# A transpose whose stores write every eighth group of four columns instead of 512 neighbouring ones

## The chip, the cores and the metric

The kernel runs on one NeuronCore of a Trainium2 chip. The metric is the device time of one execution in microseconds, lower is better. The profiled times below come from one execution recorded by the hardware profiler.

## The reference

The input is a matrix of 8192 by 8192 float32 numbers, 256 MiB. The output is its transpose.

```python
def setup_inputs():
    return {"x": np.random.randn(8192, 8192).astype(np.float32)}

def reference(x):
    return np.transpose(x)
```

Every element is read once and written once: 268.4 MB in, 268.4 MB out.

## The kernel before

**Tiling.** The input is cut into two stripes of J = 4096 columns, and each stripe into CH = 64 chunks of P = 128 rows. A chunk is thus 128 x 4096 floats, 2 MB: one row of x per partition, 16 KB each. The 128 chunks (`chunks`, line 98) are worked through in order, first all of stripe 0, then all of stripe 1.

**Loading.** `load(t)` (line 100) brings chunk t into one of three buffers `in0` to `in2`. The first three loads are issued from SP, all later ones from ACT, once PE has finished with the chunk that was in the buffer (lines 242 and 243).

**Transposing.** `transposes(k)` (line 111) works on buffer k with TensorE (PE). A chunk is divided into NR = 8 *ranges*, and each range into B = 4 transposes of 128 x 128 floats. Line 120 says which 128 columns of the chunk one transpose takes: in range q, transpose b takes the columns q * 512 + b, q * 512 + 4 + b, q * 512 + 8 + b and so on. A range is therefore 512 neighbouring columns, and after its four transposes partition p of PSUM holds the four neighbouring columns q * 512 + 4p to q * 512 + 4p + 3, 128 values of each. PSUM is used in two halves of four ranges, `ps0` and `ps1`; PE waits at line 116 until a half has been emptied, and runs in a loop of its own ("turns").

**Copying.** ACT empties the first half (ranges 0 to 3) and DVE the second (ranges 4 to 7) by copies at line 228 into blocks of the tensor `regs`. There are NREG = 9 blocks. A block holds a *window*: one range over up to W = 8 chunks in a row, so that each partition has 4 rows of the output with up to 8 * 128 = 1024 floats (4 KB) of each. The windows of the eight ranges are staggered by one chunk, so that as a rule one block becomes full with every chunk. Before a block is used again, the engine that fills it waits for the store that empties it (line 202).

**Storing.** `store(q, e, count)` (line 160) writes a full block to the output, 2 MB as a rule, with one DMA issued from ACT (line 28, inside the helper `wide_dma`; the very first store goes through line 174). Lines 166 to 168 say where. The output is a matrix of 8192 rows of 32 KB. Column j of x is row j of the output. Partition p writes the rows j0 + 4p to j0 + 4p + 3, with j0 the first column of the range. Neighbouring partitions write 4 rows, 128 KB, apart. At the passage from stripe 0 to stripe 1 a window has two parts, and its store is issued as two DMAs, one for each stripe's rows.

**Order.** ACT's instruction stream holds, for each chunk, its own copies, the stores of both halves and one load, in the order written. All of these DMAs go into one queue (q10). SP issues nothing after the first three loads and waits for the last stores at the end (line 245).

Of the kernel before, what the change touches and what calls it, by code (L numbers as in the profile page):

```python
# [24 lines left out]
def wide_dma(nc, eng, queue, out, in_):  # L25


    return eng.add_instruction(
        mybir.InstDMACopy(
            mode="Copy",  # L30
            name=nc.get_next_instruction_name(),
            engine=eng.engine,
            ins=[physical(in_)],
            outs=[physical(out)],
            queue=queue,
        )
    )
# [3 lines left out]
def kernel(  # L41
# [14 lines left out]
    P = 128  # L56
# [4 lines left out]
    S = 32  # L61
    B = 4
# [5 lines left out]
    J = S * P  # L68

    with tc.tile_critical():  # L70
        nc.alloc_sbuf_tensor("pad", [P, 32], dt)
        ident = nc.alloc_sbuf_tensor("ident", [P, P], dt).ap()
        ins = [nc.alloc_sbuf_tensor(f"in{k}", [P, J], dt).ap() for k in range(NIN)]
# [15 lines left out]
            out=ident,  # L89
# [21 lines left out]
        def transposes(k):  # L111
            nc.tensor.sem_inc(s_ld[k], -16).wait_op(s_ld[k], 16, "sem-ge")
            for q in range(NR):
                e, g = divmod(q, NH)
                if g == 0:
                    nc.tensor.sem_inc(s_bank[e], -1).wait_op(s_bank[e], 1, "sem-ge")  # L116
                for b in range(B):
                    tr = nc.tensor.transpose(  # L118
                        pss[e][:, (g * B + b) * P:(g * B + b + 1) * P],
                        ins[k][:, q * B * P + b:(q + 1) * B * P - B + b + 1:B],  # L120
                        ident,
                    )
                if q % 2:
                    tr.then_inc(s_pe, 1)
# [13 lines left out]
        with nc.body("turns", valid_engines=pe):  # L138
            now = nc.snap(turn, min_val=0, max_val=T // NIN)
            with nc.tensor.If(now < 3):  # L140
                hint = nc.tensor.mark_branch_hint_location()
            with nc.tensor.If(now > 0):
                transposes(NIN - 1)
            for k in range(NIN - 1):
                transposes(k)
            nc.regs_alu(turn, turn, 1, op=mybir.AluOpType.add)
            nc.tensor.br_lt(
                turn, T // NIN + 1, on_true="turns", on_false="done"
            ).branch_hint(hint)
# [10 lines left out]
        def store(q, e, count):  # L160
            t0, r, parts = window.pop(q)
            nc.scalar.wait_ge(s_cp[e], count)
            base = 0
            for s, a, z in parts:
                rows = (z - a) * P
                j0 = s * J + q * B * P
                dst = out[j0:j0 + B * P, a * P:a * P + rows]
                dst = dst.rearrange("(q b) i -> q b i", q=P)
                src = regs[:, r * SIZE + base:r * SIZE + base + B * rows]
                base += B * rows  # L170
                if any(stored):
                    st = wide_dma(nc, nc.scalar, "qActDynamicHW", dst, src)
                else:
                    st = nc.scalar.dma_start(
                        out=dst, in_=src.rearrange("q (b i) -> q b i", b=B)
                    )
                st.then_inc(s_st[r], 16)
                stored[r] += 1
            free.append(r)
# [5 lines left out]
        for t, (s, c) in enumerate(chunks):  # L185
            for e in range(2):
# [3 lines left out]
                for q in range(e * NH, (e + 1) * NH):  # L190
# [13 lines left out]
                    k = [p[0] for p in parts].index(s)  # L204
                    base = r * SIZE + B * P * sum(z - a for _, a, z in parts[:k])
                    _, a, z = parts[k]
# [13 lines left out]
                for u in runs:  # L220
                    off, dist = place[u[0]]
                    gap = place[u[-1]][0] - place[u[-2]][0] if len(u) > 1 else 0
                    dims = [list(regs.ap[0]), [gap, len(u)], [dist, B], [1, P]]
                    o = bass.AP(regs.tensor, regs.offset + off, dims)
                    i = pss[e][:, u[0] * B * P:(u[-1] + 1) * B * P]
                    i = i.rearrange("p (l b i) -> p l b i", b=B, i=P)
                    eng.wait_ge(s_pe, t * NH + (e * NH + u[-1]) // 2 + 1)  # L227
                    cp = nc.scalar.copy(out=o, in_=i) if e == 0 else nc.vector.tensor_copy(out=o, in_=i)  # L228
                    ends = [e * NH + g for g in u if closes(window[e * NH + g], t)]
                    if ends:  # L230
                        cp.then_inc(s_cp[e], 1)
                        copied[e] += 1
                    if u is runs[-1]:
                        if ends:
                            eng.wait_ge(s_cp[e], copied[e])
                            eng.sem_inc(s_bank[e], 1)
                        else:
                            cp.then_inc(s_bank[e], 1)
                    for q in ends:
                        store(q, e, copied[e])  # L240
# [35 lines left out]
```

## Time and profile before

| what | value |
|---|---|
| median of 3 runs | 1263.84 us (1263.76 to 1263.89) |
| span of the profiled execution | 1261.2 us |
| bytes moved by DMA | 536.97 MB |
| loads: number, size, us from issue to landing | 125 (from ACT), 2048 KB, 21.7 |
| full stores: number, size, us from issue to landing | 114, 2048 KB, 17.5 |
| copies on ACT: number, busy us | 256, 251.3 |
| copies on DVE: number, busy us | 250, 302.7 |
| DVE's idle time until PE was done | 780.2 us |
| granted TensorE clock, mean | 0.751 |

A span is the time from the first to the last instruction of the profiled execution; the times of the runs are measured around the whole execution and lie a little above it. "Busy" is the time in which an engine executes instructions; for the DMA engines it is the time their packets took. A packet is the piece of a transfer that one of the core's 16 DMA engines moves in one go; for a full load or store here it is the 16 KB of one partition. Times "to landing" count from the DMA's issue until its semaphore reports that the data has arrived, so they contain the time in the queue.

### The profile page before, as it was taken

The page shows a single profiled execution, that of the slowest core. Times are in us where ns is not written, and L with a number is a line of the kernel's source. Part 1 is how long each engine was busy: PE and PEld are TensorE (multiplying, and loading weights), DVE is VectorE, ACT ScalarE, POOL GpSimd, SP SyncE. Part 2 cuts the span into 40 slices and gives each one's busy share as a digit, 9 for nine tenths or more (in the row PEclk, how much of TensorE's full clock was granted, in tenths as well). Part 3 has the DMA queues.
Part 4 walks back from the last instruction along what each step waited for, and adds up shares of the span by engine and source line. Part 5 has one row for each costly group of instructions (what it writes and reads, how often), then busy time and mean ns, then how long its engine had stood idle before and what let it go on. Part 6 is the DMA issues. An engine that isn't in the chain of part 4 may idle for free. (4 is left out here: it accounts for less than half of the span.)

```text
span 1261.2 us, 9840 instructions
## 1 busy us (share of the span) xinstructions
PE 740.3 (59%) x4096; PEld 719.8 (57%) x4096; DVE 302.7 (24%) x250; ACT 252.6 (20%) x257; POOL 0.7 (0%) x6
## 2 busy tenths in 40 slices
PE   6555655665556565665555655656566655656561
PEld 6555555665556555655555655656566655656561
DVE  3322222222222222222222222222222222222220
ACT  3212121121111211122211121121111211122120
POOL 0000000000000000000000000000000000000000
PEclk9987867777776868687776777676867677777866
DMA  9999999999999999999999999999999999999998
GB/s 386 429 427 426 430 427 429 431 428 430 431 428 431 429 429 430 430 429 430 425 423 419 431 430 429 430 430 429 431 430 429 431 429 430 430 430 429 429 429 351
DMA packets 39273, 536.97 MB, mean 426 GB/s; under 512 B 4320, under 2 KB 4832, under 8 KB 6240
## 3 DMA queue, kind: packets, MB, share of 16 engines
q10 hardware_dynamic: 38832, 530.60, 98.9%
q1 hardware_dynamic: 432, 6.29, 1.2%
q14 instruction: 8, 0.07, 0.0%
q8 instruction: 1, 0.02, 0.0%
HBM read 268.44 MB, written 268.44 MB: 426 GB/s over the span
## 5 line engine op out<-in xcount | busy, mean ns | idle before, releaser
L118 PE MATMUL ps<-ident,in 128*128 128x128 f32 x4096 | 740.3, 363 | 492.9 <-PEq L116 492.9
L118 PEld LDWEIGHTS ps<-ident,in 128*128 128x128 f32 x4096 | 719.8, 220 | 513.2 <-issue 513.2
L228 DVE COPY regs<-ps 128x512 f32<-128x512 f32 (+3 forms) x250 | 302.7, 1246 | 932.4 <-PE ps L118 780.2
L228 ACT COPY regs<-ps 128x512 f32<-128x512 f32 (+3 forms) x256 | 251.3, 1015 | 980.9 <-PE ps L118 495.5
L228 ACT ACT_TABLE_LOAD x1 | 1.3, 1283 | 0.9 <-SPq L70 0.9
L88 POOL TENSOR_SCALAR_AFFINE_SELECT ident<-ident 128x128 f32<-128x128 f32 x1 | 0.3, 292 | 0.2 <-POOL ident L86 0.2
L86 POOL MEMSET ident<- 128x128 f32 x1 | 0.2, 204 | 0.5 <-SPq L70 0.5
L260 POOL MEMSET const-bfloat16-1.0<- 128x1 bf16 x1 | 0.1, 101 | 0.0
L260 POOL MEMSET const-uint8-127<- 128x1 uint8 x1 | 0.1, 101 | 0.0
L260 POOL MEMSET const-float32-0.0<- 128x1 f32 x1 | 0.1, 98 | 0.2 <-issue 0.2
L260 POOL MEMSET const-float32-1.0<- 128x1 f32 x1 | 0.1, 98 | 0.0
## 6 DMA issues: line engine op xcount, KB each, us to landing
in<-in_x_dram ACTq DMA_DIRECT2D x125, 2048.0 KB, 21.7
out_dram<-regs ACTq DMA_DIRECT2D x114, 2048.0 KB, 17.5
out_dram<-regs ACTq DMA_DIRECT2D x4, 1792.0 KB, 17.1
in<-in_x_dram SPq DMA_DIRECT2D x3, 2048.0 KB, 11.6
out_dram<-regs ACTq DMA_DIRECT2D x4, 1536.0 KB, 15.2
out_dram<-regs ACTq DMA_DIRECT2D x4, 1280.0 KB, 15.5
out_dram<-regs ACTq DMA_DIRECT2D x4, 1024.0 KB, 15.6
out_dram<-regs ACTq DMA_DIRECT2D x4, 768.0 KB, 16.5
```

Source lines behind the costliest of these rows:

```text
L86: nc.gpsimd.memset(ident, 0.0).then_inc(s_id, 1)
L88: nc.gpsimd.affine_select(out=ident, in_=ident, compare_op=mybir.AluOpType.not_equal, fill=1.0, base=0, pattern=[[-1, P]], channel_multipl ...
L118: tr = nc.tensor.transpose(pss[e][:, (g * B + b) * P:(g * B + b + 1) * P], ins[k][:, q * B * P + b:(q + 1) * B * P - B + b + 1:B], ident,)
L228: cp = nc.scalar.copy(out=o, in_=i) if e == 0 else nc.vector.tensor_copy(out=o, in_=i)
L260: nc = _bacc.Bacc("TRN2", target_bir_lowering=False, num_devices=1)
```

## The change

Which columns form a range is changed. Before, range q was the columns q * 512 to q * 512 + 511 of the stripe. After, it is every eighth group of four columns: partition p gets the columns p * 32 + 4q to p * 32 + 4q + 3. The step between the columns of one transpose goes from B = 4 to S = 32. The destination of the stores changes with it: neighbouring partitions write 32 rows of the output, 1 MB, apart instead of 4 rows, 128 KB. With eight partitions for each of 16 DMA engines, neighbouring engines' rows lie 8 MB apart instead of 1 MB. The four rows that one partition writes are still neighbours. The order of the work, the sizes of all instructions and transfers, the buffers and the semaphores are as before.

```diff
@@ -117,7 +117,7 @@
                 for b in range(B):
                     tr = nc.tensor.transpose(
                         pss[e][:, (g * B + b) * P:(g * B + b + 1) * P],
-                        ins[k][:, q * B * P + b:(q + 1) * B * P - B + b + 1:B],
+                        ins[k][:, q * B + b:J - S + q * B + b + 1:S],
                         ident,
                     )
                 if q % 2:
@@ -163,9 +163,8 @@
             base = 0
             for s, a, z in parts:
                 rows = (z - a) * P
-                j0 = s * J + q * B * P
-                dst = out[j0:j0 + B * P, a * P:a * P + rows]
-                dst = dst.rearrange("(q b) i -> q b i", q=P)
+                dst = out[s * J:(s + 1) * J, a * P:a * P + rows]
+                dst = dst.rearrange("(p j) i -> p j i", p=P)[:, q * B:(q + 1) * B, :]
                 src = regs[:, r * SIZE + base:r * SIZE + base + B * rows]
                 base += B * rows
                 if any(stored):
```

## The prediction

> **What bounds the kernel now.** I began with the page's busy rows, its row of slices and its DMA rows, because they say at once which resource has no idle time.
>
> ```profile
> span 1261.2 us, 9840 instructions
> PE 740.3 (59%) x4096; PEld 719.8 (57%) x4096; DVE 302.7 (24%) x250; ACT 252.6 (20%) x257; POOL 0.7 (0%) x6
> DMA  9999999999999999999999999999999999999998
> GB/s 386 429 427 426 430 427 429 431 428 430 431 428 431 429 429 430 430 429 430 425 423 419 431 430 429 430 430 429 431 430 429 431 429 430 430 430 429 429 429 351
> DMA packets 39273, 536.97 MB, mean 426 GB/s; under 512 B 4320, under 2 KB 4832, under 8 KB 6240
> q10 hardware_dynamic: 38832, 530.60, 98.9%
> HBM read 268.44 MB, written 268.44 MB: 426 GB/s over the span
> ```
>
> No compute engine is busy for more than 59% of the span. The 16 DMA engines are: digit 9 in every slice but the last, and q10, the queue that ACT issues on, alone fills 98.9% of 16 engines for the whole span. The rate stands at 427 to 431 GB/s in nearly every slice. Exactly half of the bytes are written, so half of the engines' time belongs to the stores this change moves.
>
> The chain of waits is of little use here: it reaches back over the last 2% only. So I read the waits, the forms and two stretches instead.
>
> ```profile
> ACT regs L228 <- DMA out_dram<-regs: 473.9, 60, 10.4
> PE ps L118 <- PEq L116: 492.9, 127, 8.5
> L118 PE MATMUL ps<-ident,in 128*128 128x128 f32 x4096 | 740.3, 363 | 492.9 <-PEq L116 492.9
> 300.00:600.00 300.00, 179.58 (x981) 174.55 (x979) 73.81 (x62) 59.80 (x55) 0.00 (x0) 0.74 1.01 430
> 670.00:690.00 20.00, 12.02 (x64) 11.70 (x64) 4.77 (x5) 3.73 (x2) 0.00 (x0) 0.67 1.01 414
> ```
>
> The first line: ACT, about to fill a register block again, waits 473.9 us in all for the store that empties it. The second: PE waits 492.9 us at line 116, the wait for a free half of PSUM. Line 116 is held by the copies, the copies by the stores. Everything queues behind DMA. The two stretches (engine times, then clock, DMA share, GB/s) show the DMA engines full at 430 GB/s in the steady part, and full but slower, 414 GB/s, at 670 to 690 us, where the kernel passes from the first stripe to the second.
>
> The single packet records of the trace give the price of a transfer. There are 30976 records of 16384 bytes on the two kernel queues, which is 1936 for each of 16 engines, with a mean of 614.3 ns. In the stretch 300 to 600 us their mean is 613.1 ns, and nearly all are exactly 611 or 616 ns: an engine moving at its own pace, with memory never holding it up. At 670 to 690 us the mean is 645.7 ns, because 40 of 256 records are stretched. Over the whole execution 322 records exceed 620 ns; they average 766 ns and the longest is 1689 ns. So a packet can be held up in this kernel, but it is now rare.
>
> **The change part by part.** Nothing is added or removed: 142 stores, 128 loads, 4096 transposes and 506 copies stand in the same order with the same sizes and waits. Two address patterns move.
>
> 1. Line 120, the read of the input by the transposes. The step between two columns of one transpose goes from 4 elements (16 bytes) to 32 (128 bytes). The trace has no row with a step of 128 bytes. Lower bound: 0, the 363 ns of the row stay. What hides a dearer one: in the timeline around 600 us a chunk begins every 9.76 us (600.50, 610.24, 619.99, 629.76) and its 32 transposes occupy 5.05 to 6.33 us, so about 4 us per chunk are free. The load of a later chunk is issued only when PE is done with the buffer, but a load lands 21.7 us after its issue, while 2 MB at 430 GB/s take only 4.9 us; some 16 us of queueing lie between. If the transposes became 2 us dearer per chunk, loads would be issued 2 us later into a queue that is still full. Upper bound: twice the present time, 11.2 us per chunk, past the 9.76 us cover; that is a rival below. I take 0, since at either step each column read is a place of its own.
>
> 2. Lines 166 to 168, the destination of the stores. A store writes, from each of 128 partitions, 4 neighbouring rows of the output, 4 KB of each row (8 chunks of 128 floats); a row of the output is 32 KB. Two neighbouring partitions now write 4 rows, 128 KB, apart; after the change 32 rows, 1 MB, apart. With 128 partitions over 16 engines, 8 each, neighbouring engines go from 1 MB to 8 MB apart. Source, packet sizes and number of packets stay. So the only thing that can change is how long a store packet takes at the memory. There are 268.44 MB of stores, worth 268.44e6 / 16384 / 16 = 1024 full packets per engine. As the engines have no idle time, 1 ns on each store packet is 1.02 us on the span; there is no cover at all.
>
> No row of this trace has stores 8 MB apart, so I bound the price. From below: the records can at most all fall to the steady value, 614.3 - 612.9 = 1.4 ns on 1936 packets, a gain of 2.7 us; if the third of them at 616 ns also fell to 611, 3.2 us more. I see nothing that would make them do that, but 6 us is the most there is to gain. From above: every store packet as long as the mean stretched one, 766 - 613 = +153 ns, or +157 us. The longest record would give +1100 us, but one record in 30976 is no price for all. Between them I take the row that is nearest in kind: the stretch 670 to 690 us, full queues, steady work, but another set of addresses in flight (pieces for rows of both stripes, 4096 rows or 128 MB apart, beside loads of the second). There the mean packet was 645.7 - 613.1 = 32.6 ns longer. 1024 x 32.6 ns = +33 us. I choose a price above 0 because this stretch shows that a packet's time depends on which addresses are in flight together, and the change moves the addresses of every store, to distances whose low bits are all alike.
>
> The Trainium skill, page "DMA: Bandwidth & Descriptors", section "Latency and other measured facts", speaks against this change: in copies of 128 partitions with 16 KiB each, a distance between partitions of 512 KiB gave 207 GB/s per direction, 2 MiB 164, 4 and 8 MiB 103, and a pad of 4 KiB restored 214. The 1 MiB of the changed kernel lies between its first two figures; by them, an estimate, a store packet would take 613 x 214/207 = 634 to 613 x 214/164 = 800 ns, and the span grow by 21 to 191 us. No run here shows it yet; the present 128 KB at 430 GB/s does not contradict it.
>
> Sum: 0 for line 120, +33 us for the stores, on the profiled execution's 1261.2 us: 1294.6 us. The median of the runs, 1263.84 us, is 2.6 us above that span, so I add 2.6: 1297 us.
>
> **The rivals.**
>
> *Same.* The store packets keep their 611 to 616 ns, because an engine's own pace stays the limit. For it: nearly every record of the steady part is at one of two values, so memory has some room, of unknown size; and the four rows of a packet are still 32 KB apart, and the engines are at different points of their packets, which spreads the addresses. Against it: the stretched records show that the room ends somewhere. It decides as long as the mean store packet grows by less than 2.5 ns (0.2% of 1264 us over 1024 packets). Time: 1264 us. Here belongs also that the change does not do what it says: the trace does not show which rows an engine writes, and if packets were dealt out to the engines otherwise, the distance between engines would not be what the words say. The time would be the same 1264 us.
>
> *Every store packet is held up.* All of them behave like the 322 stretched ones: +157 us, 1261.2 + 157 + 2.6 = 1420 us. For it: the distances are all powers of two, so that whatever makes two engines meet makes many meet, and always. Against it: the distance before is a power of two as well, and costs nothing. The rule of the Trainium skill quoted above leads to a time between this one and my forecast.
>
> *PE becomes the bound.* The read with 128 byte steps is slower. It decides from 9.76 us per chunk, 1.7 times the present 5.6 us. At twice: 128 x 11.2 = 1434 us; with the 8.4 us before the first transpose and the 28 us after the last (1232.9 us) 1470 us. For it: PE is the second busiest engine. Against it: a step of 16 bytes already reads scattered columns.
>
> *Faster.* The few stretched packets (70 to 230 us, mean 615.1 ns) go away: 2.7 us, 1261 us; no more than 6 us.
>
> **How the numbers follow.** Forecast, a moderate stretch around 1297 us (1267 to 1350): 0.50. Same: 0.21. Every store held up, 1350 to 1450 us: 0.20. PE bound: 0.04. Faster by over 0.2% (what a measurement of this kernel can tell from no change, 2.5 us): 0.05. So slower 0.50 + 0.20 + 0.04 = 0.74. The range runs from 1262 us, which holds the unchanged time, to 1410 us, which takes in most of the way to the case of every store held up. The likeliest case's own range is 1267 to 1350 us.
>
> **What would show it.** If I am right, the DMA digits stay at 9 in all slices while the GB/s fall from 430 to about 418 in all of them, by the same share from the first store to the last; the records of 16384 bytes are no longer all at 611 and 616 ns, and the long ones are stores; stores take longer than 17.5 us to land and ACT waits more than 473.9 us for them; the 363 ns of the transposes stay as the clock allows. I am wrong if the GB/s stay at 430 (same), if the long packets are loads, if the loss sits in a few slices only, or if the DMA digits fall while PE's rise to 9 (the read of line 120).

## The result and the profile after

The changed kernel takes 1269.62 us (median of 6 runs, 1267.28 to 1275.23) against 1263.91 us (6 runs, 1263.76 to 1264.81) for the one before. The ratio is 1.0050, 95% interval 1.0031 to 1.0069. It is slower by 5.7 us, as the sign of the forecast said, but the forecast was +33 us; that is six times too much. The changed kernel also scatters over 8 us, the one before over 1 us in these six runs; in later series single runs of the kernel before reach 1268.8 and 1277.1 us.

The page of the changed kernel, in the rows that were shown of before:

```profile
span 1266.7 us, 9840 instructions
PE 736.2 (58%) x4096; PEld 715.5 (56%) x4096; DVE 302.7 (24%) x250; ACT 253.0 (20%) x257; POOL 0.7 (0%) x6
DMA  9999999999999999999999999999999999999998
GB/s 361 391 421 428 430 429 429 428 430 430 428 430 429 429 430 429 429 429 430 429 422 420 431 429 428 428 429 430 430 429 428 429 427 429 428 430 428 424 425 361
DMA packets 39273, 536.97 MB, mean 424 GB/s; under 512 B 4320, under 2 KB 4832, under 8 KB 6240
q10 hardware_dynamic: 38832, 530.60, 98.9%
HBM read 268.44 MB, written 268.44 MB: 424 GB/s over the span
```

The DMA engines are as full as before, the bytes and packets are the same, and the span is 1266.7 us instead of 1261.2 us. The place of the loss is in the row of GB/s: 361, 391, 421 in the first three slices, where before there were 386, 429, 427; from the fourth slice on the row is nearly that of before. The two waits, and the group of the transposes:

```profile
PE ps L118 <- PEq L116: 502.7, 126, 8.5
ACT regs L227 <- DMA out_dram<-regs: 476.7, 60, 10.6
```

```profile
L118 PE MATMUL ps<-ident,in 128*128 128x128 f32 x4096 | 736.2, 363 | 502.7 <-PEq L116 502.7
```

ACT waits for its stores 476.7 us instead of 473.9 us, PE waits for PSUM 502.7 us instead of 492.9 us, and a transpose still takes 363 ns. Full stores land in 17.5 us, as before. Next the first 100 us in three stretches (columns: stretch, its length, busy us and number of PE, PEld, DVE, ACT, POOL, clock, DMA share, GB/s). First the kernel before:

```profile
0.00:30.00 30.00, 19.24 (x128) 18.77 (x128) 8.65 (x14) 9.81 (x16) 0.70 (x6) 0.94 0.94 381
30.00:60.00 30.00, 17.83 (x129) 17.18 (x128) 10.43 (x16) 8.00 (x8) 0.00 (x0) 0.94 1.02 431
60.00:100.00 40.00, 20.23 (x128) 19.58 (x128) 9.81 (x6) 7.90 (x8) 0.00 (x0) 0.87 1.00 425
```

and the changed kernel, with the two stretches that the prediction used:

```profile
0.00:30.00 30.00, 16.09 (x111) 15.66 (x112) 7.45 (x12) 8.41 (x14) 0.70 (x6) 0.93 0.95 359
30.00:60.00 30.00, 19.12 (x118) 18.49 (x117) 9.87 (x15) 7.50 (x8) 0.00 (x0) 0.78 1.00 391
60.00:100.00 40.00, 25.35 (x136) 24.70 (x135) 9.23 (x5) 8.02 (x8) 0.00 (x0) 0.71 1.01 420
300.00:600.00 300.00, 178.82 (x983) 174.00 (x984) 73.51 (x60) 59.30 (x55) 0.00 (x0) 0.73 1.01 430
670.00:690.00 20.00, 11.66 (x74) 11.18 (x72) 4.91 (x7) 4.15 (x3) 0.00 (x0) 0.81 1.01 417
```

Over the first 100 us the mean is 414 GB/s before and 393 GB/s after. The difference is 2.1 MB, which at 429 GB/s takes 4.9 us of the 5.5 us by which the spans differ. At 300 to 600 us both kernels move 430 GB/s. The records of 16384 bytes agree: their mean went from 614.3 to 616.7 ns, which on 1936 records per engine is 4.6 us. The shorter packets, most of all those of 4096 and 10240 bytes in the first stores, add 1.4 us for each engine. 873 records exceed 620 ns instead of 322, and the mean of those is 758 ns instead of 766. By number most of them stand later, but the long ones stand at the start: in the first 120 us 304 records over 620 ns average 875 ns (before 145, 807 ns). What the records of these 120 us last beyond 612.9 ns adds up to 4.8 us for each engine, of 7.3 us in the whole execution; before it was 1.6 of 2.7 us.

One more view was decisive. A DMA is shared by 16 engines, and the trace has 16 completion reports for each. The time from the first to the last of them, called drift below, tells how far the engines have come apart. Worked out from the trace's semaphore events, as a mean over the DMAs that landed in a stretch (us):

```
landed at (us)           0-15  15-30  30-45  45-60  60-75  100-150  500-600  1100-1200
before                    0.4    0.4    0.3    0.3    0.4      3.0      3.4        5.3
after                     0.4    1.8    3.3    6.1    7.5      8.0      7.4        7.6
```

Before, the 16 engines run in step for 75 us, on average within 0.4 us and never more than 0.6 us, and at 30 to 60 us they move 431 GB/s all the same. After the change they are pushed apart from the first stores on (the first is issued at some 11 us). When they are 7 to 8 us apart the loss stops (420 GB/s at 60 to 100 us, 430 GB/s later). That gave the theory to be tested.

### The profile page after: what moved, and what is told of

Read it like the earlier page. It is cut to its first block, busy times and chain, and to the rows that moved or that the text cites. A ratio compares the mean times of both kernels' runs of the same rounds, so it can differ in the third digit from the quotient of the medians.

```text
span 1266.7 us, 9840 instructions
## 1 busy us (share of the span) xinstructions
PE 736.2 (58%) x4096; PEld 715.5 (56%) x4096; DVE 302.7 (24%) x250; ACT 253.0 (20%) x257; POOL 0.7 (0%) x6
## 5 line engine op out<-in xcount | busy, mean ns | idle before, releaser
L118 PE MATMUL ps<-ident,in 128*128 128x128 f32 x4096 | 736.2, 363 | 502.7 <-PEq L116 502.7
## 6 DMA issues: line engine op xcount, KB each, us to landing
out_dram<-regs ACTq DMA_DIRECT2D x114, 2048.0 KB, 17.5
```

The source lines that it names most:

```text
L118: tr = nc.tensor.transpose(pss[e][:, (g * B + b) * P:(g * B + b + 1) * P], ins[k][:, q * B + b:J - S + q * B + b + 1:S], ident,)
```

## The experiments

**Theory A**: engines that run in step write rows 8 MB apart at the same moment; these meet at the memory and some engines are held up; once all are several us apart, they no longer meet. The loss is then paid once, at each start in step, not with each store. ("Between engines" here and below counts eight neighbouring partitions for each engine; no trace shows which rows an engine writes.) Rivals: **B**, the short stores of the first eight chunks and of the passage between stripes are dear at this distance; **C**, the read of line 120 costs; **D**, restarting from an empty queue is dear at this distance.

### Which half of the change costs

`e1_store_only` keeps the old read and takes the new destination:

```diff
-                j0 = s * J + q * B * P
-                dst = out[j0:j0 + B * P, a * P:a * P + rows]
-                dst = dst.rearrange("(q b) i -> q b i", q=P)
+                dst = out[s * J:(s + 1) * J, a * P:a * P + rows]
+                dst = dst.rearrange("(p j) i -> p j i", p=P)[:, q * B:(q + 1) * B, :]
```

> The stores' destination of the change alone; PE reads as before, so the rows of the output stand in another order. Theory A (the 16 engines begin their stores in step, rows 8 MB apart meet at the memory, the engines are pushed apart until they no longer meet): the whole of the change's cost is here, ratio 1.003 to 1.007, the first 100 us at about 393 GB/s instead of 414, and the 16 completions of one DMA are spread over 7 to 8 us from 75 us on. Theory B (short stores of the first eight chunks and of the stripe's passage are dear at this distance): the same time. Theory C (the read of line 120 costs): 1264 us as before, 414 GB/s.

`e2_read_only` is the other half:

```diff
-                        ins[k][:, q * B * P + b:(q + 1) * B * P - B + b + 1:B],
+                        ins[k][:, q * B + b:J - S + q * B + b + 1:S],
```

> The read of line 120 of the change alone; the stores go where they went before, so the rows of the output stand in another order. Theories A and B: no cost, 1264 us, ratio within 0.999 to 1.001, first 100 us at 414 GB/s, completions of one DMA within 0.5 us until 75 us. Theory C: 1268 to 1271 us.

The first 100 us of the one with the new stores alone:

```profile
0.00:100.00 100.00, 58.88 (x364) 57.30 (x365) 26.55 (x32) 23.90 (x30) 0.70 (x6) 0.84 0.99 397
```

and of the one with the new read alone:

```profile
0.00:100.00 100.00, 57.29 (x384) 55.38 (x384) 28.83 (x33) 25.73 (x32) 0.70 (x6) 0.88 0.99 414
```

The stores alone: 1267.87 us, ratio 1.0039 (1.0027 to 1.0051), 397 GB/s, and the completions 6.3 us apart at 60 to 75 us. The read alone: 1263.80 us, ratio 1.0004 (0.9995 to 1.0012), 414 GB/s, 0.9 us apart at 60 to 75 us. That last drift is more than the 0.5 us expected, without any loss. Theory C falls. Within the noise the whole cost belongs to the destination; the 1.8 us by which the stores alone stay under the full change lie inside the scatter of both.

### Bringing the engines back into step

Both kernels get four waits that let all DMA run dry, in places where only full 2 MB stores are under way:

```diff
+            if t in (24, 40, 88, 104):
+                for r in range(NREG):
+                    if stored[r]:
+                        nc.scalar.wait_ge(s_st[r], 16 * stored[r])
             if t + NIN < T:
                 nc.scalar.wait_ge(s_pe, (t + 1) * NR // 2)
```

> The kernel before, with four added waits (after chunks 24, 40, 88 and 104): ACT issues the next load only when all stores have landed, so that all 16 engines run empty and begin again in step, now with full 2 MB stores only. All theories: each drain costs its own refill, 5 to 10 us, 20 to 40 us in all; this is the control for the next run. After a drain the completions of one DMA are within 0.5 us, and spread to no more than 3 to 5 us.

> The changed kernel with the same four waits. Theory A: after each drain the engines meet again; the completions of one DMA go from under 0.5 us to 7 or 8 us within some 50 us, at a cost of 4 to 5 us each time, so this kernel is 20 to 26 us slower than the drained kernel before. Theory B: no short store follows a drain, so the distance to the drained kernel before stays 5 to 6 us and the completions stay together.

The row of GB/s of the kernel before with the waits, then the 52 us behind the first of them:

```profile
GB/s 386 428 428 427 428 427 431 344 428 429 429 425 350 426 427 426 429 430 429 427 421 413 431 430 429 430 429 339 427 428 430 429 340 429 427 429 429 429 428 364
```

```profile
258.00:310.00 52.00, 31.03 (x168) 30.03 (x166) 12.67 (x9) 11.26 (x7) 0.00 (x0) 0.74 1.01 428
```

The same of the changed kernel with the waits:

```profile
GB/s 367 400 423 428 430 432 429 317 402 416 428 430 325 391 400 427 428 425 429 426 424 417 429 430 426 429 428 292 391 402 424 430 314 395 394 424 427 419 422 366
```

```profile
258.00:310.00 52.00, 27.80 (x155) 26.80 (x153) 12.57 (x9) 9.40 (x6) 0.00 (x0) 0.70 1.01 391
```

Before: 1291.54 us, 6.9 us for each drain; the slice with the drain falls to 339 to 350 GB/s and the next is back at 426 to 428. After: 1329.72 us; behind each drain stand two or three low slices (402, 416; 391, 400; 391, 402; 395, 394), as at the start. The distance between the two kernels is 38.2 us instead of 5.7 us. The four drains thus cost the changed kernel 32.5 us more, 8.1 us each. In its trace the completions of the first DMA after the first drain, a load, are 0.5 us apart, those of the next, a store, 3.7 us, and 7 to 8 us some 70 us later; in the drained kernel before they go from 0.6 us to 0.8 us in the same time. Theory B falls as the sole cause, because no short store is near the first drain. A cost of writing rows for the first time is excluded as well: the first stores of every range come in the first eight chunks, so all rows of stripe 0 had been written to, in other columns, by chunk 24. Theory A has the direction right, and its size too low: I had expected 4 to 5 us each time.

### Starting out of step

To tell A from D the engines are put out of step at the start. Nine small copies behind the first three loads (41 rows in all; the 48 in the expectation is a miscount) are meant to occupy only some of the engines:

```diff
+        for rows, times in ((8, 3), (4, 3), (2, 2), (1, 1)):
+            for _ in range(times):
+                nc.sync.dma_start(out=skew[at:at + rows, :], in_=x[at:at + rows, 0:J]).then_inc(s_dm, 16)
+                at += rows
```

> The kernel before with nine small extra copies (48 rows of 16 KB in all, from x into a scratch) on SP's queue right after its three loads: three of 8 rows, three of 4, two of 2 and one of 1 row, meant to occupy only some of the 16 engines each, so that the engines come out of the first 15 us apart by up to 5.5 us instead of in step. Control for the next run. All theories: the late engines end later, 1264 to 1270 us; completions of one DMA spread over 4 to 6 us from 20 us on.

> The changed kernel with the same nine copies. Theory A (engines in step meet): those already apart don't meet, and of the 120 pairs of engines only the 35 that are still in step do; the distance to the control shrinks from 5.7 us to 0 to 3 us, and the first 100 us are within 1 to 8 GB/s of the control's. Theory D (what the drains showed is a cost of restarting from an empty queue at this distance, not of being in step): the distance to the control stays 5 to 7 us.

First 100 us of the control, then of the changed kernel with the copies:

```profile
0.00:100.00 100.00, 60.42 (x376) 58.84 (x377) 26.56 (x32) 23.86 (x30) 0.70 (x6) 0.85 0.99 409
```

```profile
0.00:100.00 100.00, 59.05 (x369) 57.33 (x370) 26.56 (x32) 23.89 (x30) 0.70 (x6) 0.84 0.99 403
```

The copies do what they should: the completions of the loads and stores are 4.9 and 4.6 us apart at 30 to 45 us. The trace has 16 packets of 1 KB for the one-row copy, so that one was split over the engines; the other eight did the work. The control takes 1267.01 us, the changed kernel 1269.02 us (1.0031, 1.0006 to 1.0056, against the plain kernel before; the control 1.0023, 1.0010 to 1.0035). The distance shrinks from 5.7 us to 2.0 us, and in the first 100 us from 21 to 6 GB/s. The queue of the stores starts as empty as ever here, so D does not explain what has gone; being in step does. For the 2.0 us that remain D is not excluded. The changed kernel with the copies is even no slower than without them, though it moves 0.7 MB more.

### How the loss depends on the distance

Three other distances and one that is no power of two. Theory A is split here into A1 and A2, as the first expectation says. Of each edit only the lines with the stores' destination are shown. The first is an edit of the kernel before, the other three of the changed kernel; those with 256 KB and 4 MB also change the columns that line 120 reads, to fit. `e5_near_rows` (256 KB between engines):

```diff
-                dst = dst.rearrange("(q b) i -> q b i", q=P)
+                dst = dst.rearrange("(b q) i -> q b i", q=P)
```

> The kernel before with rows dealt out another way: in range q, partition p writes the rows q*512 + p, + 128, + 256, + 384, so neighbouring partitions write neighbouring rows (32 KB apart) and neighbouring engines rows 256 KB apart; PE reads 128 neighbouring columns. The output is the reference's. Theory A1 (what makes the engines meet are the high address bits, more the farther apart their rows are): the engines never meet, the completions of one DMA stay within 0.6 us to the end, no more than 414 GB/s in the first 100 us, and the last engine ends up to 3 us earlier: 1260 to 1264 us. Theory A2 (any distance that is a power of two is as bad as another once engines are in step): spread and time as in the changed kernel, 1268 to 1272 us.

`e6_rows_4mb`:

```diff
+                h = q // 4
+                dst = out[s * J + h * 2048:s * J + (h + 1) * 2048, a * P:a * P + rows]
+                dst = dst.rearrange("(p j) i -> p j i", p=P)[:, q % 4 * B:(q % 4 + 1) * B, :]
```

> A range is every fourth group of four columns in one half of the stripe: neighbouring partitions 512 KB, neighbouring engines 4 MB apart, half of the change's distance. The output is the reference's. Theory A1: between before and after, 1265 to 1268 us, first 100 us at 400 to 412 GB/s, completions spread over 4 to 7 us by 100 us. Theory A2: as after, 1269 us.

`e7_rows_16mb`:

```diff
+                dst = out[:, a * P:a * P + rows].rearrange("(p j) i -> p j i", p=P)
+                dst = dst[:, s * S + q * B:s * S + (q + 1) * B, :]
```

> The changed kernel with the rows of both stripes interleaved, 32 of every 64, so that neighbouring partitions write 2 MB, neighbouring engines 16 MB apart, twice the change's distance; the rows of the output stand in another order. Theory A1: worse than after: 1275 to 1300 us, first 100 us under 385 GB/s, spread over 10 us; by the Trainium skill's page on DMA (section on latency and other measured facts), whose 2 MiB row gives 164 GB/s where 214 is full, an estimate is up to 1450 us if the engines never get out of each other's way. Theory A2: as after, 1269 us.

`e8_padded`:

```diff
+                step = 32 * M + 1024 if s == 0 else 28 * M
+                at = q * B * M if s == 0 else (4608 + q * B) * M
...
+                dst = bass.AP(out.tensor, out.offset + at + a * P, [[step, P], [M, n], [1, rows]])
```

> The changed kernel with stripe 0's stores at a distance of 1 MB + 4 KB between partitions (8 MB + 32 KB between engines), no power of two, written as shifted pieces; stripe 1's partitions are 28 rows (896 KB) apart, and its range 7 stores only 3 of its 4 rows, 4.2 MB less in all, worth 9.8 us. The output is not the transpose. Theory A1 and the page's padding rule (a pad of 4 KiB brings back the full rate): no meeting: first 100 us at 414 GB/s, completions within 1 us until 75 us, 1252 to 1256 us. If the distance itself matters and not its low bits: first 100 us at 393 GB/s, spread to 7 us by 75 us, 1258 to 1262 us.

First 100 us with 256 KB:

```profile
0.00:100.00 100.00, 60.70 (x384) 58.40 (x384) 28.85 (x33) 25.91 (x32) 0.70 (x6) 0.84 0.99 409
```

with 4 MB:

```profile
0.00:100.00 100.00, 61.00 (x378) 59.41 (x379) 26.65 (x32) 24.83 (x32) 0.70 (x6) 0.83 0.99 403
```

with 16 MB, and the passage between the stripes; the third line is the passage of the kernel before:

```profile
0.00:100.00 100.00, 56.82 (x352) 55.06 (x352) 25.23 (x32) 23.01 (x30) 0.70 (x6) 0.83 0.99 376
600.00:720.00 120.00, 64.32 (x352) 62.54 (x352) 27.00 (x38) 21.95 (x26) 0.00 (x0) 0.73 1.01 395
600.00:720.00 120.00, 69.14 (x384) 67.20 (x384) 29.03 (x36) 23.89 (x27) 0.00 (x0) 0.74 1.01 424
```

and with 8 MB + 32 KB:

```profile
0.00:100.00 100.00, 58.61 (x384) 56.69 (x384) 28.84 (x33) 25.74 (x32) 0.70 (x6) 0.86 0.99 408
```

```
between engines  median us  ratio (95% interval)       GB/s 0-100 us   drift (us) at 30-45, 60-75, 100-150
256 KB           1264.59    1.0011 (1.0000 to 1.0022)  409             0.7   1.8   2.1
1 MB (before)    1263.55    1                          414             0.3   0.4   3.0
4 MB             1265.34    1.0009 (1.0000 to 1.0018)  403             0.9   2.2   3.1
8 MB (after)     1269.62    1.0050 (1.0031 to 1.0069)  393             3.3   7.5   8.0
16 MB            1285.65    1.0185 (1.0156 to 1.0215)  376             7.7   6.4   7.8
8 MB + 32 KB     1255.94    0.9932 (0.9914 to 0.9949)  408             0.9   1.7   2.1
```

The ratios compare each run with the kernel before of its own series; the row of 8 MB comes from the first series. GB/s and drift are those of one profiled execution each.

From 4 MB up the loss grows with the distance: 2, 6, 22 us by the medians, and 11, 21, 38 GB/s in the first 100 us. The first of these, like the 1 us at 256 KB, has an interval that touches 1, so only 8 and 16 MB are clear of noise. Theory A2 falls: 16 MB costs much more than 8 MB, and 1 MB nothing while the engines are in step.

The rest of A1 missed in its details. At 256 KB the engines drift more at first than at 1 MB and the time is no better, so nearer is not simply better. At 4 MB the drift reaches 3 us by 100 us, not 4 to 7 us. At 16 MB the drift at the start goes no farther than 8.4 us, not over 10 us as expected; but the loss occurs a second time, at the passage, where the rate falls to 395 GB/s against 424 GB/s before. That is 3.5 MB, worth some 8 us of the 22 us, about as much as the start (3.8 MB, some 9 us). Theory A as it stands does not explain this second loss, since the engines were 6.7 us apart when it began. At the passage each window is stored as two short DMAs, and their packets are among those that are stretched (those of 4096 bytes take 226 ns, before 163 ns). So for the passage at 16 MB theory B, short stores, remains possible.

With the pad the bytes left out are worth 9.8 us; 1263.55 less 9.8 is 1253.7 us, so by the medians 2.2 us of a loss remain where the changed kernel has 5.7 us, with 408 GB/s instead of 393. The interval of the four runs reaches from 1252.7 to 1257.1 us, so it does not show whether anything remains. That the row distance is an exact power of two makes up most of the loss of the changed kernel, by the medians; whether it makes up all of it stays open.

The Trainium skill, page "DMA: Bandwidth & Descriptors", section "Latency and other measured facts", gives 164 GB/s of 214 for 2 MiB between partitions, the distance of the run with 16 MB between engines; taken as a price on every store this was an estimate of up to +191 us, and the run shows +22 us. Its remark that a pad of 4 KiB brings back the rate agrees in the main with the padded run, 408 GB/s in the first 100 us where the changed kernel has 393 and the kernel before 414. It puts the slowdown down to streams in lock-step that share memory channels, as an inference; the drained and the skewed runs bear out the lock-step, and no run here shows the channels.

### Loads at a large distance

```diff
-                out=ins[t % NIN], in_=x[c * P:(c + 1) * P, s * J:(s + 1) * J]
+                out=ins[t % NIN], in_=x.rearrange("(p r) m -> p r m", p=P)[:, c, s * J:(s + 1) * J]
```

> The kernel before with its loads at a large distance: chunk c takes row c of each group of 64 rows of x, so neighbouring partitions read 2 MB and neighbouring engines 16 MB apart, as the stores did in the run with 16 MB; the stores stay as before. The columns of the output stand in another order. If reads meet as writes do: slower by 10 to 30 us, first 100 us under 395 GB/s. If only writes meet: 1262 to 1266 us, 414 GB/s.

```profile
0.00:100.00 100.00, 56.63 (x353) 54.88 (x354) 26.56 (x32) 23.80 (x30) 0.70 (x6) 0.86 0.97 385
600.00:720.00 120.00, 69.93 (x388) 67.98 (x387) 29.24 (x39) 23.96 (x28) 0.00 (x0) 0.74 1.01 423
```

1271.08 us, ratio 1.0051 (1.0034 to 1.0069), 385 GB/s, and the completions 1.4 us apart already among the first loads, 6.2 us at 60 to 75 us. Reads show the same picture as writes: a loss at the start, a growing drift, then the full rate (no drain or skewed start was tried on them). At 16 MB they cost 7.5 us, less than the 10 to 30 us I had expected, and a third of what stores cost at that distance. In the first 100 us they lose 29 GB/s, not far from the 38 of the stores; the difference is mostly the passage, where these loads lose nothing (423 against 424 GB/s).

## Why the prediction was right in sign and wrong in size

**What bounds the kernel.** Right: the DMA engines have no idle time, and what a packet takes longer is seen in the span nearly one for one (4.6 us in the records of 16384 bytes and 1.4 us in the shorter ones, 5.5 us in the span).

**Line 120 at 0.** Right, and measured by itself: 1.0004 (0.9995 to 1.0012). The rival "PE becomes the bound" falls with it.

**The price of a store packet.** This is the step that failed: "1024 x 32.6 ns = +33 us". The row that I took it from, 670 to 690 us, holds a disturbance that lasts 20 us, and I charged it to every store of the execution. Nor did that disturbance grow with the change: in the same stretch of the changed kernel the mean record is 638.2 ns, before it was 645.7 ns. In the steady part (230 to 590 us) a 16 KB record takes 613.5 ns after (138 of 9433 over 620 ns) and 613.1 ns before (22 of 9438). Spread over all 1024 stores the measured price is 4.6 us / 1024 = 4.5 ns. The mistake lies in the form, a price for each packet; the cost is in the main a sum paid once, until the engines have come apart. The trace of before showed how such a cost behaves. Most of its 322 stretched records stood in bursts (the start, 70 to 230 us, the passage, the end), with exact 611 and 616 ns records between them. A cost that lasts would not be expected to leave such a pattern. I read the bursts for their height alone, not for what ended them.

**The price above zero.** Right in its reason, that addresses in flight together decide; but the row that it was read from did not show this for the distance, so the sign was in part luck. The trace of before could also have told me about the step: its completions drift in two jumps, 0.4 to 3.0 us and later to 5.3 us, and I did not look at them. For the rival "same" the prediction took the engines to be "at different points of their packets"; at the start they are within 0.4 us of each other, less than the 611 ns of one packet.

**The signs named beforehand.** The full DMA digits, the 363 ns of the transposes, more long records and a longer wait of ACT for its stores (476.7 instead of 473.9 us) came true. An even fall of the GB/s to 418 did not; the text named "if the loss sits in a few slices only" as the sign of being wrong, and that is what happened. Stores landing later than 17.5 us did not come true either. Whether the long records are stores cannot be read from the records, which give queue, size and time but not the direction; e1_store_only shows that the stores' addresses bring them about.

**The rivals.** "Same" is excluded by the interval, though only 5.7 us away; "every store held up" is 150 us away. By theory A it would need the engines to stay in step, and at this distance they do not; four forced restarts bring the changed kernel 38 us behind its control. The prediction's estimate of +21 to +191 us makes 1285 to 1455 us, wider than "a time between this one and my forecast" (1420 and 1297 us); the measured 1269.62 us lies under all of it.

**What stays open.** That the engines meet at the memory is inferred from the distances and the pad; what there makes rows at these distances meet was not tried. Why a drain costs 8.1 us and the start some 5 us, and why 2.0 us remain with the skewed start (by its plan 35 of 120 pairs of engines stay in step; the trace does not name engines), is not settled. Nor is the second loss of the run with 16 MB, at the passage. That the scatter of the changed kernel (1267.28 to 1275.23 us) comes from chance in how the engines come apart is an argument, not shown; single runs of the kernel before lie up to 13 us above their median too.

## What to carry to other kernels

Where a DMA-bound kernel sends its engines to rows a large power of two apart (8 MB and more here), ask first whether they run in step, and what brings them back into step: here the cost was paid at the start and again at every drain, so a kernel with many barriers would pay many times what one long stream pays once. A slow stretch of the trace gives the height of a cost; what ended it tells whether to multiply it by all packets. The first-to-last time of the 16 completions of a DMA shows directly whether the engines are in step.

## What the runs showed of the hardware

The 16 DMA engines can run in step for 75 us (0.4 us on average) and move the full rate, 431 GB/s at 30 to 60 us before. Once disturbed they stay apart, in the quiet parts by a constant amount (3.4 us from 200 to 600 us before); after the first 150 us only the drains brought all of them back within 0.6 us. In the changed kernel the loss at the start ended by itself once the engines were 7 to 8 us apart, more than the 4.9 us that a 2 MB transfer takes at 430 GB/s; with the new stores alone 6 to 7 us were enough. Stores and loads both lose at a distance of 16 MB: 22 us in stores, of which some 9 at the start, and 7.5 us in loads.
